# One decay matrix per head: both scan directions summed before the exp, and added before the product

## The chip, the core and the metric

The kernel runs on one core of one Trainium2 chip. The metric is the device time of one execution in microseconds (us). Three runs of the kernel before took 1930.81, 1932.88 and 1936.28 us, with a median of 1932.88 us.

## The reference, cut to what matters

The program has two blocks. The first is a bidirectional state-space (SSD) mixer with a Fourier mixer beside it; the second holds two layers of attention, each followed by an expert-choice feed-forward. The change lies in the SSD scan of the first block. 24 heads in four groups of six scan 256 tokens in two chunks of 128, forward and backward:

```
a_cum = jnp.cumsum(a, axis=-1)          # a = dt * A, per head and direction
lmat = jnp.exp(segsum(a))               # 128 x 128 decays of a chunk, lower triangle, else 0
cb = jnp.einsum('bclgn,bcsgn->bgcls', cc, bc)
y_diag = jnp.einsum('bgcls,bgrcls,bcsgrp->bclgrp', cb, lmat, xc)   # xc = x * dt
...
y_f, h_f = ssd_chunked(xs, dt_f, A[0], bm, cm, h0_f)
y_b, h_b = ssd_chunked(flip(xs), flip(dt_b), A[1], flip(bm), flip(cm), h0_b)
y = y_f + flip(y_b) + d_skip.astype(f32).reshape(g, r)[:, :, None] * xs
```

In unflipped order the forward decays fill one triangle of a head's 128 x 128 matrix and the backward decays the other. The two meet on the diagonal, where both are 1.

## The kernel before, in words

Tokens are on partitions for the scan: a tile [128, ...] holds the 128 positions s of a chunk. `tri` holds four 0/1 triangles. `a` holds dt * A by chunk, direction and head. `cb` holds C B^T of a chunk, masked by each direction's triangle. `mt` holds the decays, and after the masking the matrices that multiply x.

`decay_group` (L746 to L761) builds the decays of a group, per chunk c and direction d:

- L752 multiplies the triangle by `a`, giving six 128 x 128 blocks in a tile `w3` (768 columns), on POOL for forward and on DVE for backward.
- L754 calls `split` (L197): ACT copies the tile into float32r (L203), and the rest is a subtraction (L205) that goes to DVE twice and to POOL once in every three calls. Both parts land in a tile of `hring`, which has four buffers. Every projection of the kernel splits its weights through the same four buffers and the same turn of engines.
- L757 and L758 sum by a product with the triangle `trr`, in two halves of 384 columns and with two parts each, and ACT takes the exp into `mt` (L759).

`ssd_group` (L763) then uses them. `mask` (L785) multiplies `mt` by `cb` on DVE, one instruction of 768 columns per chunk and direction. L799 and L810 make x * dt for both directions on POOL (`weighted`, L768, 768 columns). L825 multiplies per chunk, head and direction, 24 products a group that accumulate two by two in `py`. The compiler turns each of these float32 products into two matmul instructions.

Python generators set the order: `weave` (L851) emits the projections of the next group (`dense_group`) with 1.3 or 1.7 steps of the chain "scan of this group, output part of the group before, decays of the next group" after each of its steps. A scheduler then moves instructions by a simulated timeline, so the final order on each engine is not the written one. The last group is woven with the projections of layer 0's context (`even_dense`), whose input tiles E are written at L450 and L451. Each engine takes its queue in order.

Of the kernel before, what the change touches and what calls it, by code (L numbers as in the profile page):

```python
# [24 lines left out]
F32 = mybir.dt.float32  # L25
# [11 lines left out]
def _constants():  # L37
# [11 lines left out]
    # Fourier: 64-point over the channels of a group, 256-point over the sequence, ortho norm  # L49
# [50 lines left out]
    ex = np.zeros((128, 2, 2, 2), f)   # [kind: query decay, ctx weight][tile][direction]  # L100
# [13 lines left out]
def kernel(ctx, tc, A, out, dbg=None):  # L114
# [14 lines left out]
    def banks(**n):  # L129
        """Split the banks of PSUM anew: tiles of a tag go around its n[tag] banks."""  # L130
# [9 lines left out]
    def psa():  # L140
        return ps_("a")
# [39 lines left out]
    def load_w(src, parts, k0=0, k=8):  # L181
        """A ring tile [128, k, n]: rows (k0..k0+k, p) of src, and its column ranges (c0, n) side by side."""
# [14 lines left out]
    def split(wv):  # L197
        """A part of a ring tile as the sum of two float32r parts."""
# [9 lines left out]
    def mm3(o, l, r, start, stop):  # L208
        """A product of operands in two float32r parts each."""
        mm(o, l[0], r[0], start, False)  # L210
        mm(o, l[0], r[1], False, False)
        mm(o, l[1], r[0], False, stop)
# [6 lines left out]
    def products(wv, outs, first=True, last=True):  # L219
        """Products over the rows of a ring tile; outs: (psum, f), f(k, weights of chunk k) = (stationary, moving)."""  # L220
# [15 lines left out]
    def as_rows(yT, c0, n, k0=0):  # L236
        """f of products: weights' columns c0..c0+127 stationary, the first n tokens of yT moving."""
        return lambda k, w: (cut(w, ALL, slice(c0, c0 + 128)), cut(yT, ALL, k0 + k, n if isinstance(n, slice) else slice(0, n)))

    def as_cols(yT, t, k0=0, c=ALL):  # L240
        """f of products: token tile t of yT stationary, the weights' columns c moving."""
        return lambda k, w: (cut(yT, ALL, k0 + k, slice(128 * t, 128 * t + 128)), cut(w, ALL, c))

# [14 lines left out]
    def tr_at(o, i):  # L258
        """Transpose to other partitions than 0: a product with the identity."""
# [30 lines left out]
    def conditions(i, names, engs):  # L290
        """silu of the two streams' conditions of a pair, as columns."""
# [57 lines left out]
    def ada_early(l, s, slots):  # L349
        """Load the weights of a later modulation step into given slots."""  # L350
# [8 lines left out]
    def ada(src, s, pair, cols, bias, between=None, bank=None, ws=None):  # L359
        """Columns s*512.. of silu(c) @ w + b for both streams of a pair, in chunks of 128: into cols."""  # L360
# [30 lines left out]
    def diag(col, h):  # L391
        """The identity's columns by half h of a gate's columns col [128, 8]: [128, (4, 128)]."""
# [5 lines left out]
    def gate_bcast(o, col, h):  # L398
        """o [128, 512] = half h of a gate on all partitions."""
# [5 lines left out]
    powed = [None]  # L405

    def rstd(ss, n, width, q=None):
        """(ss / width + EPS) ** -0.5"""
# [1411 lines left out]
```

## Time and profile before

| what | value |
|---|---|
| median of three runs | 1932.88 us |
| profiled execution: span from first to last instruction | 1930.3 us |
| PE busy | 1669.9 us (87%) |
| DVE busy | 803.8 us (42%) |
| ACT busy | 520.6 us (27%) |
| POOL busy | 350.4 us (18%) |
| loads from HBM | 554.16 MB, 288 GB/s over the span |

The page gives no time of the profiled execution apart from its span; the three runs lie 0.5 to 6.0 us above that span. The span falls into stages: the first block to about 475 us, layer 0's attention to about 770 us, its experts to 1160 us, layer 1's attention to about 1410 us and its experts to the end. The shares in the table are means over stages that are limited by different things, so the stage that holds the change has to be read by itself.

### The profile page before, as it was taken

To read this page: it belongs to the slowest core of one execution; us is meant where nothing else is said; L and a number is where in the kernel's file an instruction comes from. 1 tells how busy PE (TensorE), PEld (TensorE's weight loads), DVE (VectorE), ACT (ScalarE), POOL (GpSimd) and SP (SyncE) were. 2 spreads that over 40 slices of the span, in tenths; PEclk is the share of its full clock that TensorE was granted. 3 is DMA by queue.
4 is the path that set the end of the run, shared out by engine and by line. 5 is a ranking of instruction groups with operands and counts; after the bars stand their busy time and mean duration, and the time that the engine had idled before them with its cause. 6 is when DMAs were issued, how large, how long until landed. Compare 5 with 4: busy or idle time off the path is not lost.

```text
span 1930.3 us, 29195 instructions
## 1 busy us (share of the span) xinstructions
PE 1669.9 (87%) x12132; PEld 1041.4 (54%) x12132; DVE 803.8 (42%) x1523; ACT 520.6 (27%) x1024; POOL 350.4 (18%) x294
## 2 busy tenths in 40 slices
PE   5999999899999999899989998779998966666665
PEld 4787787799888678433333322268785522222221
DVE  4537788857645664332232121165654300000002
ACT  4334545535443443211210000062532200000001
POOL 3114545553422411000000000032310000000001
PEclk8999999999999999899999999999997976766767
DMA  9566443546566628999989999952287999999996
GB/s 340 194 225 217 159 131 126 184 144 214 190 204 186 210 106 320 355 346 409 409 339 409 410 409 409 407 183 72 90 332 278 408 409 409 409 409 408 409 408 269
DMA packets 223016, 557.11 MB, mean 289 GB/s; under 512 B 23531, under 2 KB 80199, under 8 KB 222884
## 3 DMA queue, kind: packets, MB, share of 16 engines
q1 hardware_dynamic: 216608, 547.92, 75.9%
q10 hardware_dynamic: 5732, 6.26, 1.0%
q8 instruction: 95, 1.56, 0.3%
q0 software_dynamic: 544, 1.06, 0.1%
q14 instruction: 37, 0.30, 0.0%
HBM read 554.16 MB, written 1.05 MB: 288 GB/s over the span
## 4 chain that ended last, share of the span: by engine, by line
PE 59%; DMA 26%; DVE 8%; ACT 3%; issue 2%; POOL 1%; SPq 0%; POOLq 0%; DVEq 0%; ACTq 0%
PE ps_a L149 47%; DMA wm<-in_moe_w_dram 23%; PE ps_b L149 7%; PE ps_b L256 3%; DVE wh L205 2%; DMA w<-in_w_in_dram 1%; PE ps_g L149 1%; DMA w<-in_w_ada_dram 1%; ACT wh L203 1%; DVE pr L1392 1%; DVE ye L1311 1%; DVE hid L1293 0%; DMA w<-in_w_out_dram 0%; DMA w<-in_even_w_in_dram 0%; DVE acc L611 0%
## 5 line engine op out<-in xcount | busy, mean ns | idle before, releaser
L149 PE MATMUL ps_a<-wm,xf 128*32 128x256 f32 (+1 forms) x1792 | 286.4, 575 | 74.6 <-DMA wm<-in_moe_w_dram 72.9
L149 PE MATMUL ps_a<-wm,hidT 128*32 128x256 f32 (+1 forms) x1536 | 204.6, 507 | 45.5 <-DMA wm<-in_moe_w_dram 29.3
L149 PEld LDWEIGHTS ps_a<-wm,xf 128*32 128x32 f32 (+1 forms) x1792 | 91.3, 141 | 259.7 <-issue 131.2
L203 ACT ACTIVATE wh<-w 128x1024 fp32r<-128x1024 f32 (+3 forms) x168 | 165.1, 993 | 177.6 <-PE ps_a L149 104.9
L205 POOL TENSOR_TENSOR wh<-w,wh 128x1024 fp32r<-128x1024 f32 (+3 forms) x56 | 132.3, 2362 | 336.9 <-ACT wh L203 298.3
L205 DVE TENSOR_TENSOR wh<-w,wh 128x1024 fp32r<-128x1024 f32 (+3 forms) x112 | 156.8, 1402 | 73.3 <-ACT wh L203 73.0
L1293 DVE TENSOR_TENSOR hid<-hid,ps_a 128x512 f32<-128x512 f32 (+1 forms) x32 | 17.7, 554 | 382.6 <-PE ps_a L149 382.6
L149 PEld LDWEIGHTS ps_a<-wm,hidT 128*32 128x32 f32 (+1 forms) x1536 | 68.8, 129 | 153.7 <-issue 72.0
L1311 DVE TENSOR_TENSOR ye<-ps_a,SC 32x512 f32<-32x512 f32 (+1 forms) x128 | 70.8, 553 | 184.0 <-PE ps_a L149 182.4
L1210 POOL TENSOR_TENSOR Pg<-Pg,CV 128x128 f32<-128x128 f32 x24 | 9.5, 422 | 750.2 <-DVE Pg L1208 750.2
L1291 ACT ACTIVATE hid<-ps_a 128x512 f32<-128x512 f32 (+1 forms) x32 | 15.7, 489 | 478.7 <-PE ps_a L149 456.6
L149 PE MATMUL ps_a<-hT,wh 128*128 128x512 f32 (+1 forms) x672 | 136.6, 360 | 5.2 <-ACT hT L496 5.1
L149 PEld LDWEIGHTS ps_a<-hT,wh 128*128 128x128 f32 x672 | 111.2, 197 | 24.6 <-ACT hT L496 5.5
L149 PE MATMUL ps_a<-E,wh 128*128 128x256 f32 x768 | 101.3, 286 | 6.5 <-DVE E L451 5.3
L149 PE MATMUL ps_a<-wm,xe 128*32 128x256 f32 (+1 forms) x768 | 104.2, 482 | 0.7 <-ACT hid L1291 0.5
L149 PE MATMUL ps_a<-wh,E 128*128 128x256 f32 (+1 forms) x576 | 99.4, 324 | 2.6 <-DVE wh L205 1.4
L149 PEld LDWEIGHTS ps_a<-E,wh 128*128 128x128 f32 x768 | 94.3, 191 | 12.0 <-DVE E L451 5.9
L149 PEld LDWEIGHTS ps_a<-wh,E 128*128 128x128 f32 x576 | 80.9, 188 | 15.4 <-issue 4.7
L149 PE MATMUL ps_a<-wm,ye 128*32 128x256 f32 x512 | 49.7, 526 | 26.3 <-DMA wm<-in_moe_w_dram 26.3
L611 DVE SCALAR_TENSOR_TENSOR acc<-ps_a,CV,acc 128x189 f32<-128x189 f32 (+2 forms) x160 | 65.8, 426 | 15.6 <-ACT acc L600 13.3
L1011 ACT ACTIVATE pr<-ps_a,nb 128x512 f32<-128x512 f32 (+1 forms) x80 | 47.8, 600 | 79.9 <-DVE nb L1008 71.4
L149 PE MATMUL ps_a<-w,SC 128*32 128x128 f32 x1728 | 65.3, 287 | 3.2 <-DMA w<-in_w_ada_dram 2.1
(522 smaller groups left out, 2430.6 us busy)
## 6 DMA issues: line engine op xcount, KB each, us to landing
wm<-in_moe_w_dram SPq DMA_DIRECT2D x382, 1024.0 KB, 18.3
w<-in_ada_w_dram SPq DMA_DIRECT2D x46, 1024.0 KB, 6.1
w<-in_even_w_in_dram SPq DMA_DIRECT2D x24, 1024.0 KB, 6.9
w<-in_w_ada_dram SPq DMA_DIRECT2D x12, 1024.0 KB, 9.0
w<-in_w_in_dram SPq DMA_DIRECT2D x8, 1024.0 KB, 7.8
w<-in_even_w_out_dram SPq DMA_DIRECT2D x8, 1024.0 KB, 6.4
w<-in_w_in_dram SPq DMA_DIRECT2D x12, 512.0 KB, 7.2
w<-in_w_in_dram SPq DMA_DIRECT2D x8, 768.0 KB, 4.4
```

The costliest lines, as they stand in the source:

```text
L149: PE.matmul(o, l, r, start=start, stop=stop, **kw)
L203: S.activation(hv, wv, AF.Copy)
L205: (G if flip_lo[0] == 0 else V).tensor_tensor(lo, wv, hv, op=OP.subtract)
L256: PE.transpose(o, i, ident[:n, :n])
L611: V.scalar_tensor_tensor(o, xi[:, r0 + dr:r1 + dr, c0 + dc:c1 + dc], tap(i, j), o, op0=OP.mult, op1=OP.add)
L1011: S.activation(pr[:, :n], ps[:, :n], AF.Exp, bias=nb, scale=scale, accum_out=su)
L1210: G.tensor_tensor(g_, g_, bcast(AFF[s][:, t, e4, None], [128, 4, 32]), op=OP.mult)
L1291: S.activation(hid, p1[:, :N], AF.Silu)
L1293: V.tensor_tensor(hid, hid, p3[:, :N], op=OP.mult)
L1311: V.tensor_tensor(ye[o:o + 32, s, N * j:N * j + N], py[i:i + 32, :N], G2[i:i + 32, :], op=OP.mult)
L1392: V.scalar_tensor_tensor(pr[0][0][:, :n], pr[1][0][:, :n], rc, pr[0][0][:, :n], op0=OP.mult, op1=OP.add)
```

## The change

The sums of `a` are split into two float32r parts once, in `ah`, for all groups, instead of splitting each product of `a` with a triangle. POOL multiplies the triangle by the high part, DVE by the low part, straight into an `hring` tile. The sums of both directions accumulate in the same PSUM columns, four products per half, and one exp serves both: one triangle holds the forward decays and the other the backward ones, so `mt` has six blocks per chunk instead of twelve. In `mask`, ACT scales the forward `cb` by dt per head and DVE adds the backward `cb` times its dt, into a tile `w3` of six blocks; one instruction of 768 columns multiplies `mt` by it. The product then takes one matrix per head and x itself; the tiles x * dt and `weighted` on them are gone.

```diff
+    ah = [sp.tile([128, 2, 48], F32R, name=f"ah{i}") for i in range(2)]
...
+        V.tensor_copy(ah[0], a[:, 0:2])
+        V.tensor_tensor(ah[1], a[:, 0:2], ah[0], op=OP.subtract)
...
     def decay_group(g):
         for c in range(2):
+            parts = []
             for d in range(2):
-                w3 = wk.tile([128, 2, 384], F32, name="w3")
-                w = w3.rearrange("p a (r l) -> p (a r) l", l=128)
+                hi_tags.append(hi_tags.pop(0))
+                t = hring.tile([128, 2, 1024], F32R, name="wh", tag=hi_tags[0])
                 h = 24 * d + 6 * g
-                (V if d else G).tensor_tensor(w, bcast(tri[:, d, None, :], [128, 6, 128]),
-                                              bcast(a[:, c, h:h + 6, None], [128, 6, 128]), op=OP.mult)
-                hi, lo = split(w3)
                 for i in range(2):
-                    ps = psa()
-                    mm(ps[:, 0:384], trr[:, d], hi[:, i], start=True, stop=False)
-                    mm(ps[:, 0:384], trr[:, d], lo[:, i], start=False, stop=True)
-                    S.activation(GA["mt"][:, c, 6 * d + 3 * i:6 * d + 3 * i + 3],
-                                 ps[:, 0:384].rearrange("p (a b) -> p a b", a=3), AF.Exp)
-                yield
+                    (V if i else G).tensor_tensor(t[:, i, 0:768].rearrange("p (r l) -> p r l", l=128),
+                                                  bcast(tri[:, d, None, :], [128, 6, 128]),
+                                                  bcast(ah[i][:, c, h:h + 6, None], [128, 6, 128]), op=OP.mult)
+                parts.append(t)
+                if d == 0:
+                    yield
+            for i in range(2):
+                ps = psa()[:, 0:384]
+                n = 0
+                for d in range(2):
+                    for j in range(2):
+                        mm(ps, trr[:, d], parts[d][:, j, 384 * i:384 * i + 384], start=n == 0, stop=n == 3)
+                        n += 1
+                S.activation(GA["mt"][:, c, 3 * i:3 * i + 3], ps.rearrange("p (a b) -> p a b", a=3), AF.Exp)
+            yield
...
         def mask(c):
-            m = GA["mt"][:, c].rearrange("p (d r) l -> p d r l", d=2)
-            for d in range(2):
-                V.tensor_tensor(m[:, d], m[:, d], bcast(cb[:, c, d, None, :], [128, 6, 128]), op=OP.mult)
+            w = wk.tile([128, 2, 384], F32, name="w3").rearrange("p a (r l) -> p (a r) l", l=128)
+            for r in range(6):
+                h = 6 * g + r
+                S.activation(w[:, r], cb[:, c, 0], AF.Copy, scale=dt[:, c, h:h + 1])
+                V.scalar_tensor_tensor(w[:, r], cb[:, c, 1], dt[:, c, 24 + h:25 + h], w[:, r], op0=OP.mult, op1=OP.add)
+            V.tensor_tensor(GA["mt"][:, c], GA["mt"][:, c], w, op=OP.mult)
...
-        xd = {0: weighted(bcast(hd(xs[:, 0])[:, None], [128, 2, 6, 64]), heads(dt[:, 0], g))}
...
-                xd[1] = weighted(bcast(hd(xs[:, 1])[:, None], [128, 2, 6, 64]), heads(dt[:, 1], g))
...
             for r in range(6):
-                for d in range(2):
-                    mm(py[:, 64 * r:64 * r + 64], GA["mt"][:, c, 6 * d + r], xd[c][:, d, 64 * r:64 * r + 64],
-                       start=d == 0, stop=d == 1)
+                mm(py[:, 64 * r:64 * r + 64], GA["mt"][:, c, r], xs[:, c, 64 * r:64 * r + 64])
```

The order of the DMA issues on SP's queue is the same in both kernels. On the other engines the scheduler's order differs in many places from the first group on. Two of them matter below.

The first is DVE's queue at the start of the last group, beside the first tiles E of layer 0's context. Before, E is the float32r remainder that PE's projections wait for (L451), `cb` and `mt` are the masks (L779, L785), and `wh` are the remainders of split weights (L205):

```order
L205 TENSOR_TENSOR wh<-w,wh 128x1024
L448 TENSOR_SCALAR r<-ps_b,MS,M_0_82 128x256
L779 TENSOR_TENSOR cb<-ps_b,kb 128x256 x2
L785 TENSOR_TENSOR mt<-mt,cb 128x768 x3
L205 TENSOR_TENSOR wh<-w,wh 128x1024
L785 TENSOR_TENSOR mt<-mt,cb 128x768
L451 TENSOR_TENSOR E_3446<-r,E_3445 128x512
L804 TENSOR_TENSOR hs<-hs,ps_b 128x384 x2
L817 TENSOR_TENSOR y<-ps_b,ea 128x384
L451 TENSOR_TENSOR E_3446<-r,E_3445 128x512
```

In the changed kernel, L791 is the former L779, L800 the new scaled sum of the two halves of `cb`, and L801 its product with `mt`:

```order
L448 TENSOR_SCALAR r<-ps_b,MS,M_0_82 128x256
L791 TENSOR_TENSOR cb<-ps_b,kb 128x256 x2
L205 TENSOR_TENSOR wh<-w,wh 128x1024 x2
L451 TENSOR_TENSOR E_3410<-r,E_3409 128x512 x2
L800 SCALAR_TENSOR_TENSOR w_3468<-cb,dt,w_3468 128x128 x6
L801 TENSOR_TENSOR mt<-mt,w_3468 128x768
L1353 TENSOR_TENSOR lp<-lp 128x2x64
L800 SCALAR_TENSOR_TENSOR w_3673<-cb,dt,w_3673 128x128
L831 TENSOR_TENSOR y<-ps_b,ea 128x384
L800 SCALAR_TENSOR_TENSOR w_3673<-cb,dt,w_3673 128x128 x5
L205 TENSOR_TENSOR wh<-w,wh 128x1024
L801 TENSOR_TENSOR mt<-mt,w_3673 128x768
```

The four masks that stood ahead of E are gone from there; both halves of E now stand ahead of the new mask of either chunk.

The second is POOL's queue in the first group. Before, `w<-kb,a` is the triangle times `a` (L752), `w<-xs,ws` and `w<-xs,dt` are `weighted` (L768), and `wh<-w` are remainders of splits:

```order
L205 TENSOR_TENSOR wh<-w,wh 128x1024 x2
L205 TENSOR_TENSOR wh<-w,wh 128x768 x2
L752 TENSOR_TENSOR w_1552<-kb,a 128x768
L205 TENSOR_TENSOR wh<-w_1552,wh 128x768
L768 TENSOR_TENSOR w_1620<-xs,ws 128x768
L768 TENSOR_TENSOR w_1622<-xs,ws 128x768
L768 TENSOR_TENSOR w_1701<-xs,ws 128x768
L205 TENSOR_TENSOR wh<-w,wh 128x1024
L768 TENSOR_TENSOR w_1704<-xs,dt 128x768
L798 TENSOR_TENSOR hs<-h_1619,ea 128x768
```

In the changed kernel L759 is the triangle times the high part, and L780 is `weighted`:

```order
L205 TENSOR_TENSOR wh<-w,wh 128x1024 x2
L205 TENSOR_TENSOR wh<-w,wh 128x768
L780 TENSOR_TENSOR w_1608<-xs,ws 128x768
L780 TENSOR_TENSOR w_1610<-xs,ws 128x768
L205 TENSOR_TENSOR wh<-w,wh 128x768
L759 TENSOR_TENSOR wh<-kb,ah_473 128x768 x4
L780 TENSOR_TENSOR w_1701<-xs,ws 128x768
L814 TENSOR_TENSOR hs<-h_1607,ea 128x768
```

The four products of the first group stand in one block behind two `weighted` and a remainder, and one `weighted` is gone.

## Rows read from the trace of the kernel before

**Rows 1.** Stretches: busy us (and instructions) per engine, clock, DMA share, GB/s
```profile
150.00:475.00 325.00, 307.77 (x2133) 262.99 (x2133) 248.62 (x363) 164.60 (x265) 161.20 (x99) 0.97 0.52 165
460.00:770.00 310.00, 301.38 (x2490) 244.02 (x2488) 182.93 (x385) 134.06 (x306) 95.88 (x85) 0.99 0.61 202
770.00:1160.00 390.00, 362.45 (x1635) 137.32 (x1636) 112.57 (x242) 52.62 (x127) 9.06 (x16) 0.98 0.98 386
```

**Rows 2.** The page's chain that ended last, by engine
```profile
PE 59%; DMA 26%; DVE 8%; ACT 3%; issue 2%; POOL 1%; SPq 0%; POOLq 0%; DVEq 0%; ACTq 0%
```

**Rows 3.** PE's waits from 150 to 475 us: total us, times, longest
```profile
PE ps_a L149 <- DVE E L451: 4.9, 1, 4.9
PE ps_b L256 <- DVE gy L833: 3.9, 4, 1.6
PE ps_a L149 <- ACT mt L759: 3.5, 2, 3.3
```

**Rows 4.** PE in order of time: start us, us, instructions
```profile
203.08 2.79 PE L149 MATMUL ps_b<-w,mt 128*128 128x64 f32 x24
```

**Rows 5.** Line L752 of the kernel: ns min/median/max, first and last start
```profile
L752 POOL TENSOR_TENSOR w<-kb,a x8: 1467/1472/1472, 83.9 to 356.5; 128x768 f32<-128x768 f32 x8
L752 DVE TENSOR_TENSOR w<-kb,a x8: 942/1104/2554, 84.3 to 366.4; 128x768 f32<-128x768 f32 x8
```

**Rows 6.** Groups by form, 150 to 475 us, DVE and POOL
```profile
L611 DVE SCALAR_TENSOR_TENSOR acc<-ps_a,CV,acc 128x189 f32<-128x189 f32 x64 | 25.7, 408 | 13.4 <-ACT acc L600 12.8
...
L785 DVE TENSOR_TENSOR mt<-mt,cb 128x768 f32<-128x768 f32 x16 | 25.4, 1615 | 1.1 <-ACT mt L759 1.0
L205 DVE TENSOR_TENSOR wh<-w,wh 128x768 fp32r<-128x768 f32 x22 | 25.1, 1142 | 8.8 <-ACT wh L203 8.8
...
L205 POOL TENSOR_TENSOR wh<-w,wh 128x768 fp32r<-128x768 f32 x10 | 19.2, 1924 | 31.1 <-ACT wh L203 31.1
...
L768 POOL TENSOR_TENSOR w<-xs,dt 128x768 f32<-128x768 f32 x8 | 16.1, 2010 | 5.5 <-PE ps_b L256 2.8 <-PE ps_b L149 2.7
...
L374 DVE TENSOR_TENSOR M<-ps_b,BC 128x8 f32<-128x8 f32 x8 | 1.3, 163 | 6.9 <-PE ps_b L256 6.9
```

**Rows 7.** Groups by form, 150 to 475 us, ACT
```profile
L203 ACT ACTIVATE wh<-w 128x768 fp32r<-128x768 f32 x32 | 26.7, 844 | 22.5 <-PE ps_a L149 10.7 <-DMA w<-in_w_in_dram 6.9 <-POOL w L752 3.6
...
L759 ACT ACTIVATE mt<-ps_a 128x384 f32<-128x384 f32 x32 | 14.9, 499 | 1.8 <-PE ps_a L149 1.5
...
L759 ACT ACT_TABLE_LOAD x5 | 6.4, 1283 | 0.1
...
L841 ACT ACTIVATE xg<-ps_b,VC 128x256 fp32r<-128x256 f32 x12 | 4.9, 477 | 1.2 <-PE ps_b L256 0.7 <-PE ps_a L149 0.5
...
L156 ACT ACTIVATE ra<-ps_a 128x128 f32<-128x128 f32 x4 | 1.1, 267 | 2.1 <-PE ps_a L149 2.1
```

**Rows 8.** DVE in order of time, 369 to 390 us
```profile
374.89 4.71 DVE L785 TENSOR_TENSOR mt<-mt,cb 128x768 f32<-128x768 f32 x3
...
381.94 2.23 DVE L785 TENSOR_TENSOR mt<-mt,cb 128x768 f32<-128x768 f32 x1
384.09 2.82 DVE L451 TENSOR_TENSOR E<-r,E 128x512 fp32r<-128x512 f32 x1
```

**Rows 9.** PE in order of time, where the second group's projections begin
```profile
174.10 6.88 PE L149 MATMUL ps_a<-hT,wh 128*128 128x512 f32 x28
```

**Rows 10.** POOL in order of time, first group
```profile
158.01 1.85 POOL L205 TENSOR_TENSOR wh<-w,wh 128x768 fp32r<-128x768 f32 x1 [5.83 <-ACT wh L203]
...
163.19 1.84 POOL L205 TENSOR_TENSOR wh<-w,wh 128x768 fp32r<-128x768 f32 x1 [0.96 <-ACT wh L203]
```

**Rows 11.** SP's queue: first loads of the experts' weights
```profile
726.97 4.68 SPq L1241 DMA_DIRECT2D wm<-in_moe_w_dram  x6
```

**Rows 12.** What SP's queue waited for, 470 to 800 us
```profile
SPq L1241 <- PE ps_a L149: 41.1, 11, 13.7
```

**Rows 13.** DVE in order of time, first group
```profile
163.30 2.55 DVE L752 TENSOR_TENSOR w<-kb,a 128x768 f32<-128x768 f32 x1
```

More of the change, by code (lines that the diff above doesn't have):

```diff
@@ L873, in open_wm @@
         GA["wm"] = enter(b1, name="b1m", bufs=1, reuse_waits="tile")
-        GA["mt"] = GA["wm"].tile([128, 2, 12, 128], F32, name="mt")
+        GA["mt"] = GA["wm"].tile([128, 2, 6, 128], F32, name="mt")
         yield
```

## The prediction

> **What bounds the kernel now.** I first read the busy time by stretches, to see which engine fills the stage that holds the change. From 150 to 475 us, where all four groups are scanned, PE is busy 307.77 of 325 us, at a granted clock of 0.97 and a DMA share of 0.52; DVE is busy 248.62 us, ACT 164.60 and POOL 161.20 [rows 1]. So the stage is PE's, DVE comes second, and DMA has room. The chain that ended last says the same of the whole program: PE holds 59% of it, DMA 26%, DVE 8% [rows 2]. PE's waits in this stage come next, since idle PE is the only other thing that can be won here. All its idle time is 325 - 307.77 = 17.2 us. The largest single wait is 4.9 us for E, DVE's remainder of layer 0's context; four waits for the normalized output gy make 3.9 us, and two for the exps 3.5 us, of which one is 3.3 us [rows 3].
>
> **PE's work.** Before, a group has 24 products of `mt` with x * dt, and each is two instructions; 24 instructions, that is one chunk, took 2.79 us [rows 4]. The change halves them: 12 instructions fewer in each of 4 x 2 chunks, 96 in all. At 2.79 / 24 = 0.116 us each they are 11.2 us. PE's sums with `trr` stay 64 instructions in number; only their grouping in PSUM differs. As PE is full around these products, I count the 11.2 us in whole. If PE had to wait there for something else, they would be worth nothing: 0 to -11.2.
>
> **DVE, POOL and ACT.** DVE loses 16 masks of 1.615 us (25.8), 8 triangle products (median 1.104 us, 8.8), and of the subtractions of 768 columns 13 of 22 by the order (13 x 1.142 = 14.8) [rows 5, 6]: 49.4 us. It gains 16 triangle products (17.7), 8 full masks (8 x 1.615 = 12.9), 48 small sums of 128 columns, and three subtractions of 1024 columns, because the turn of `split` shifts; I price these at no less than the 768 columns' 1.142 (3.4). The trace has no such small sum. The nearest rows are 408 ns for 189 columns of the same operation and 163 ns for 8 columns of an addition [rows 6], so 7.8 to 19.6 us for all; by columns between them, 0.326 us and 15.6 us. DVE gains 49.6 us: even, with ends of -8 and +4.
>
> POOL loses 8 triangle products (1.472), 8 `weighted` on dt (2.010) and 3 remainders of 768 columns (1.924), 33.6 us, and gains 16 products, 23.6 us: 10 us less [rows 5, 6]. ACT loses 16 copies of 768 columns (0.844) and 16 exps (0.499), 21.5 us, and gains 48 scaled copies of 128 columns. The nearest are 267 ns for a plain copy of 128 and 477 ns for 256 with a scale per partition [rows 7]; I take 0.36, 17.3 us, with ends of 12.8 and 22.9. None of this sets the end by itself. It matters only where PE waits, and I go through those places.
>
> **The wait for E goes.** Ahead of E, DVE does three masks in 4.71 us, a remainder, and the fourth mask in 2.23, and only then E, at 384.09 [rows 8]. In the changed order both halves of E stand ahead of either mask. E is ready 4.71 + 2.23 = 6.9 us sooner on DVE, and PE's wait of 4.9 [rows 3] is shorter than that, so I count -4.9. What is late next is POOL's and ACT's part of E, on engines that lose work; and if the group's two new products on DVE run long, the wait stays in part: 0 to -4.9. The masks that move behind E are then needed by the scan's products, and PE has projections in between.
>
> **The first group.** Here PE's wait of 3.3 us for an exp [rows 3] falls, and its run of projections of the second group starts at 174.10 [rows 9]. Before, each decay passes four steps (product, copy, remainder, sum); now two. But now all four high parts stand in one block on POOL behind two `weighted` and a remainder. From 158.0, where POOL's remainder starts before [rows 10], this is 2 x 2.010 + 1.924 + 4 x 1.472 = 11.8 us [rows 5, 6], so until 169.8; PE's last sums with `trr` and their exps come about 2 us later. I take a start of 172, -2 us, with ends of 0 (every product slowed to the 2.01 of `weighted`, +2.2) and -4.
>
> **What it adds.** The order has two more loads of ACT's function table, at 1.283 us each [rows 7], both in the second group, ahead of the exps and of gy's part. Fewer copies and exps stand beside them, so I count +1 of 2.6. There the wait for gy is already the second largest [rows 3]. The Trainium skill, "ScalarE: Activation LUTs", section "What ACT_TABLE_LOAD costs", puts a switch at 2.66 us with the drain; by that the two would be up to 5.3 us and the sum 2.7 us later at most, while the row shows the load alone. Further, a tile of `hring` is now held from the forward product to the end of both directions' sums, where projections need the same four buffers: +1, with an end of +9 that stands among the rivals.
>
> **The sum.** -11.2 - 4.9 - 2 + 1 + 1 = -16.1 us. The profiled execution would go from a span of 1930.3 to 1914.2; the median of the runs lies 2.6 us above the span, so I predict 1917 us.
>
> The later stages should pass the gain on. Layer 0's attention is PE's too, 301.38 of 310 us with a DMA share of 0.61, and the experts' loads that fill the next stage (DMA 0.98) [rows 1] are first issued at 726.97 [rows 11], by a line whose longest waits are for PE, 41.1 us [rows 12]; they begin as much sooner as PE gets there.
>
> **Rivals.**
>
> *All of PE's idle time in the stage closes too.* POOL's relief speaks for it, gy's wait against it, since gy hangs on a chain of DVE, ACT and POOL that keeps its length. -11.2 - 17.2 = -28.4: 1904.5 us.
>
> *The held buffers give half of it back.* A projection's split must then wait for a sum of both directions. One late split costs PE a copy and a remainder, 0.844 + 1.924 = 2.8 us by [rows 6, 7], at most; half of that in each of the six woven chunks is +9 over my +1 less: 1917 + 8 = 1925 to 1926. The order, which puts the next projections' copies ahead of exps in places, speaks for it; the four buffers and PE's long runs against it.
>
> *DVE and POOL block each other: slower.* The high and low products of a direction become ready together, and both engines read SBUF for them. Before, one DVE product took 2.55 us [rows 13] while POOL worked on a remainder [rows 10], against 0.942 us at best [rows 5]. If all the new pairs ran like this, the 12 DVE products of the three stretches in which DVE stands before PE (the first group, the third's start, the fourth's start) grow by 12 x (2.55 - 1.10) = 17.4 us. The wait for E then stays, as do 2 us for loads and buffers and 3 us of the small sums' upper end: -11.2 + 17.4 + 2 + 0 to 3 = +8 to +11, 1941 to 1944 us. It decides against any gain from a mean of about 1.9 us per product: 9.2 / 12 above 1.10. POOL's 10 us less and the median of 1.104 beside much POOL work speak against it. The Trainium skill, "SBUF — State Buffer", section "Who interferes with whom", says that a DVE instruction with two SBUF inputs contends with a GpSimd instruction that reads SBUF and that the later one is blocked entirely; the row of 2.55 us agrees, and the rule speaks for this rival.
>
> *It doesn't reach the end.* The experts' loads could hang on something that doesn't move with PE, and the stage full of DMA would then start as before: 1932 us. SP's waits for PE [rows 12] speak against it.
>
> **How the numbers follow.** A measurement of this kernel can tell about 0.3%, 5.8 us, from no change: faster is below 1927.1, slower above 1938.7. The forecast (1911 to 1923) gets 0.55, all idle closed 0.10, the held buffers 0.20, of which a third lands within 0.3%, blocking 0.10, and no effect at the end 0.05. Faster: 0.55 + 0.10 + 0.13 = 0.78; same: 0.07 + 0.05 = 0.12; slower 0.10. The range of 1905 to 1931 leaves out the slower rival and little else.
>
> **What would show it.** In the profile after: products of x with `mt`, 12 instructions in about 1.4 us; PE's wait for E gone; the second group's projections at about 172; DVE's products of `ah` at a mean under 1.9 us; the first load of experts' weights near 711. Wrong would be PE idle by much more than 17 us between 150 and 460, with waits for DVE or POOL at the decays, or the first expert load at 727 as before.

## The result, and the profile after

The changed kernel takes 1910.32 us (median of four runs, 1906.99 to 1914.0) where the kernel before, on the same chip, takes 1934.58 us. The ratio is 0.9877, with a 95% interval of 0.9852 to 0.9901. A second measurement of the changed kernel on another chip gave 0.9896 (0.9873 to 0.9919). It is faster by 20 to 24 us; the forecast was 16. The profiled span goes from 1930.3 to 1905.1 us.

The busy time by stretches, as in [rows 1]: the stretch from 150 to 475 us, then layer 0's attention and its experts.

```profile
150.00:475.00 325.00, 307.56 (x2160) 264.75 (x2159) 262.73 (x423) 174.37 (x300) 156.42 (x98) 0.98 0.54 176
460.00:770.00 310.00, 298.34 (x2466) 236.45 (x2465) 176.41 (x407) 125.44 (x297) 86.18 (x80) 0.98 0.63 215
770.00:1160.00 390.00, 364.49 (x1573) 132.08 (x1571) 104.86 (x209) 48.05 (x115) 9.05 (x16) 0.99 0.98 387
```

PE is as full as before. Since the program now is some 18 us ahead there, the first window holds more work of layer 0, so it can't be subtracted from [rows 1]; lengths between the same instructions can, and a table below gives them. DVE has 262.73 us where it had 248.62, but most of that is the later work: up to the scan's end, the first product of `dg` with `ones`, DVE is busy for 282.8 us before (at 428.6 us) and 286.2 after (at 410.4). The chain that ended last is the same in kind as in [rows 2]:

```profile
PE 60%; DMA 26%; DVE 8%; ACT 3%; issue 2%; POOL 1%; SPq 0%; DVEq 0%; POOLq 0%; ACTq 0%
```

PE's waits from 150 to 475 us, as in [rows 3] (total us, times, longest):

```profile
PE ps_a L149 <- DVE wh L205: 6.1, 4, 2.5
PE ps_b L149 <- DVE hs L819: 3.3, 2, 1.7
PE ps_a L149 <- DVE E L451: 1.8, 2, 1.3
PE ps_b L256 <- DVE gy L845: 1.8, 2, 1.5
PE ps_a L149 <- ACT E L450: 1.8, 2, 0.9
PE ps_a L149 <- POOL wh L759: 1.7, 2, 1.3
```

The one wait of 4.9 us for E and the one of 3.3 us for an exp are gone. In their place stand shorter waits for split weights (`wh`), for the states' sums `hs` and for both parts of E. The products of x with one matrix per head, against [rows 4]; the start of the second group's projections, against [rows 9]; and SP's first load of experts' weights, against [rows 11]:

```profile
197.83 1.45 PE L149 MATMUL ps_b<-xs,mt 128*128 128x64 f32 x12
```
```profile
168.53 1.86 PE L149 MATMUL ps_a<-hT,wh 128*128 128x512 f32 x7
```
```profile
706.98 3.12 SPq L1253 DMA_DIRECT2D wm<-in_moe_w_dram  x6
```

Groups by form, 75 to 475 us on DVE and POOL, 150 to 475 us on ACT, against [rows 5 to 7] (count | busy us, mean ns | idle before):

```profile
L800 DVE SCALAR_TENSOR_TENSOR w<-cb,dt,w 128x128 f32<-128x128 f32 x48 | 32.5, 737 | 0.0
L759 DVE TENSOR_TENSOR wh<-kb,ah 128x768 fp32r<-128x768 f32 x16 | 24.3, 1526 | 0.4 <-PE ps_a L149 0.4
L801 DVE TENSOR_TENSOR mt<-mt,w 128x768 f32<-128x768 f32 x8 | 7.6, 955 | 0.2
...
L759 POOL TENSOR_TENSOR wh<-kb,ah 128x768 fp32r<-128x768 f32 x16 | 32.3, 2039 | 6.2 <-PE ps_a L149 6.2
...
L799 ACT ACTIVATE w<-cb,dt 128x128 f32<-128x128 f32 x48 | 14.9, 391 | 3.9 <-DVE mt L801 2.6 <-PE ps_b L149 1.3
L772 ACT ACT_TABLE_LOAD x6 | 7.7, 1283 | 0.1
```

The 48 small sums (L800) take 32.5 us. The means of this view can hold more than an instruction's own work, so the same line by itself, with minimum, median and maximum in ns:

```profile
L800 DVE SCALAR_TENSOR_TENSOR w<-cb,dt,w x48: 337/347/2498, 166.3 to 377.5; 128x128 f32<-128x128 f32 x48
```

Of the 48, 33 take 0.34 to 0.35 us. The other 15 take 0.60 to 2.50, and by the single records each of these 15 ends 0.14 to 0.15 us behind the end of a POOL instruction (in x0 it is 15 of 15 again). The largest case is seen in time. DVE and POOL at the last group's first mask:

```profile
364.85 7.65 DVE L800 SCALAR_TENSOR_TENSOR w<-cb,dt,w 128x128 f32<-128x128 f32 x6
372.54 0.96 DVE L801 TENSOR_TENSOR mt<-mt,w 128x768 f32<-128x768 f32 x1
...
377.80 1.21 DVE L205 TENSOR_TENSOR wh<-w,wh 128x1024 fp32r<-128x1024 f32 x1
...
380.14 1.00 DVE L819 TENSOR_TENSOR hs<-hs,ps_b 128x384 f32<-128x384 f32 x2
```
```profile
364.34 1.50 POOL L394 TENSOR_TENSOR dg<-kb,M 128x512 f32<-128x512 f32 x1
365.80 1.34 POOL L451 TENSOR_TENSOR E<-r,E 128x512 fp32r<-128x512 f32 x1
367.10 1.09 POOL L394 TENSOR_TENSOR dg<-kb,M 128x512 f32<-128x512 f32 x1
368.15 2.46 POOL L205 TENSOR_TENSOR wh<-w,wh 128x1024 fp32r<-128x1024 f32 x1
370.57 1.53 POOL L814 TENSOR_TENSOR hs<-h,ea 128x768 f32<-128x768 f32 x1
```

Six sums of 0.35 us take 7.65, as long as five POOL instructions back to back: the first five end with one POOL instruction each (the fourth runs from 368.26 to 370.76, POOL's remainder beside it from 368.15 to 370.61), and the sixth, with POOL idle, takes 0.34. In the first group six took 7.46 us from 166.27, beside POOL; the next six, with POOL idle, took 1.66:

```profile
176.98 1.66 DVE L800 SCALAR_TENSOR_TENSOR w<-cb,dt,w 128x128 f32<-128x128 f32 x6
```

### The profile page after: what moved, and what is told of

Same layout as the page of the kernel before. It is cut to its first block, busy times and chain, and to the rows that moved or that the text cites. A ratio compares the mean times of both kernels' runs of the same rounds, so it can differ in the third digit from the quotient of the medians.

```text
span 1905.1 us, 29062 instructions
## 1 busy us (share of the span) xinstructions
PE 1652.3 (87%) x12036; PEld 1026.2 (54%) x12036; DVE 794.4 (42%) x1563; ACT 519.3 (27%) x1042; POOL 335.1 (18%) x288
## 4 chain that ended last, share of the span: by engine, by line
PE 60%; DMA 26%; DVE 8%; ACT 3%; issue 2%; POOL 1%; SPq 0%; DVEq 0%; POOLq 0%; ACTq 0%
PE ps_a L149 48%; DMA wm<-in_moe_w_dram 22%; PE ps_b L149 7%; PE ps_b L256 3%; DMA w<-in_w_in_dram 2%; DVE w L800 1%; PE ps_g L149 1%; DMA w<-in_w_ada_dram 1%; DVE wh L205 1%; ACT wh L203 1%; DMA w<-in_w_out_dram 1%; DVE ye L1323 1%; DVE pr L1404 1%; DVE hid L1305 1%; DVE acc L614 1%
## 5 line engine op out<-in xcount | busy, mean ns | idle before, releaser
L149 PE MATMUL ps_a<-wm,xf 128*32 128x256 f32 (+1 forms) x1792 | 280.0, 558 | 73.6 <-DMA wm<-in_moe_w_dram 71.8
L149 PE MATMUL ps_a<-wm,hidT 128*32 128x256 f32 (+1 forms) x1536 | 211.8, 529 | 47.4 <-DMA wm<-in_moe_w_dram 31.7
L203 ACT ACTIVATE wh<-w 128x1024 fp32r<-128x1024 f32 (+3 forms) x152 | 151.7, 1007 | 164.6 <-PE ps_a L149 99.9
L1305 DVE TENSOR_TENSOR hid<-hid,ps_a 128x512 f32<-128x512 f32 (+1 forms) x32 | 17.7, 555 | 375.2 <-PE ps_a L149 375.2
L205 POOL TENSOR_TENSOR wh<-w,wh 128x1024 fp32r<-128x1024 f32 (+3 forms) x50 | 116.0, 2321 | 304.4 <-ACT wh L203 278.5
L205 DVE TENSOR_TENSOR wh<-w,wh 128x1024 fp32r<-128x1024 f32 (+3 forms) x102 | 135.2, 1329 | 71.9 <-ACT wh L203 71.4
```

The costliest lines, as they stand in the source:

```text
L149: PE.matmul(o, l, r, start=start, stop=stop, **kw)
L203: S.activation(hv, wv, AF.Copy)
L205: (G if flip_lo[0] == 0 else V).tensor_tensor(lo, wv, hv, op=OP.subtract)
L1305: V.tensor_tensor(hid, hid, p3[:, :N], op=OP.mult)
```

## The experiments

The x runs were timed in five rounds beside the kernel before. The lengths (us) come from one profile each, as differences between the starts of the same four events: c_n's load on SP, the start of the second group's projections, the first transpose of c_n on PE, and the first product of `dg` with `ones` behind the scan (before: 155.8, 174.1, 369.2, 428.6). The four together are the scan's stage; "first", "middle" and "last" are its parts.

| kernel | ratio to before (95%) | first | middle | last | stage |
|---|---|---|---|---|---|
| before | 1 | 18.3 | 195.1 | 59.4 | 272.8 |
| x5, new turn in before | 0.9974 (0.9956 to 0.9993) | 18.2 | 194.9 | 59.8 | 273.0 |
| after | 0.9877 (0.9852 to 0.9901) | 15.9 | 183.8 | 58.1 | 257.8 |
| x0, after again | 0.9896 (0.9873 to 0.9919) | 16.0 | 183.4 | 58.6 | 257.9 |
| x4, old turn after scan | 0.9897 (0.9879 to 0.9916) | 15.8 | 185.2 | 58.5 | 259.4 |
| x1, products twice | 0.9940 (0.9922 to 0.9958) | 16.0 | 189.2 | 62.8 | 268.0 |
| x2, decays alone | 0.9940 (0.9921 to 0.9959) | 16.0 | 191.0 | 61.7 | 268.8 |
| x3, products alone | 1.0007 (0.9986 to 1.0029) | 18.1 | 191.8 | 60.6 | 270.4 |
| x6, states before mask | 0.9927 (0.9908 to 0.9946) | 16.1 | 186.4 | 57.2 | 259.7 |
| x7, low and high on DVE | 0.9913 (0.9895 to 0.9932) | 14.1 | 190.0 | 57.0 | 261.1 |
| x8, first group on DVE | 0.9911 (0.9890 to 0.9932) | 14.0 | 190.7 | 58.0 | 262.8 |
| x9, own tile | 0.9891 (0.9872 to 0.9911) | 14.6 | 189.6 | 51.3 | 255.5 |
| x10, no small sums | 0.9867 (0.9843 to 0.9891) | 16.1 | 181.7 | 50.1 | 247.9 |
| x12, sum on POOL | 0.9906 (0.9880 to 0.9933) | 15.6 | 183.6 | 53.3 | 252.5 |

The pairs with the same code up to there (before and x5; after, x0 and x4) agree within 0.2 and 1.7 us, so a difference of 2 us or more in the stage is taken as one of the kernel.

**x0, the changed kernel again.** No edit.

> The changed kernel once more, beside the others on one chip, with a second profile. All theories: 1907 to 1914 us. If the 2.9 us by which its profile was ahead before 150 us, where no instruction of the change runs, are the clock's doing and not the change's, this profile has them in part or not at all; if they are the order's, they are there again.

1910.43 us, and the stage's 257.9 us repeats the first profile's 257.8. The lead ahead of the scan is there again too: c_n's load comes at 152.4 us (155.8 before, 152.7 in the first profile). That does not make it the order's, since x5, whose code there is that of before, has it as well (152.8).

**x1, every product twice.**

```diff
+                for _ in range(2):
-                mm(py[:, 64 * r:64 * r + 64], GA["mt"][:, c, r], xs[:, c, 64 * r:64 * r + 64])
+                    mm(py[:, 64 * r:64 * r + 64], GA["mt"][:, c, r], xs[:, c, 64 * r:64 * r + 64])
```

> The changed kernel with each of its 48 products of x with the decay matrix issued twice into the same columns, the second overwriting the first: 96 matmul instructions more, nothing else written differently. Theory A (PE's instructions in this stage count in full): 96 x 0.116 = 11.2 us slower than the changed kernel, 1921 to 1922 us. Rival B (the gain comes from waits around the decays, and PE has slack at the products): 0 to 3 us slower, 1910 to 1913 us. Rival C (the gain comes from the scheduler's other order): the order moves again, so anything between 1905 and 1935, and not the same as A by more than chance.

1919.08 us, 8.7 over the changed kernel; the stage grows by 10.2. PE's busy time in its middle and last part:

```profile
168.50:352.30 183.80, 175.90 (x1260) 144.82 (x1259) 159.50 (x293) 95.81 (x169) 88.06 (x59) 0.99 0.49 156
352.30:410.40 58.10, 52.34 (x349) 47.41 (x348) 40.96 (x52) 30.76 (x55) 32.21 (x21) 0.94 0.54 177
```
```profile
168.50:357.70 189.20, 182.23 (x1330) 151.35 (x1330) 160.86 (x294) 95.68 (x169) 87.50 (x59) 1.00 0.47 151
357.70:420.50 62.80, 57.39 (x374) 52.22 (x373) 38.14 (x50) 30.89 (x55) 32.93 (x21) 0.89 0.49 166
```

The first pair is the changed kernel, the second x1: 70 and 25 instructions more, 6.3 and 5.1 us more of PE; in the last part some of this is the lower clock (0.89 against 0.94). This is theory A, if short of its 11.2: the products reach the end nearly in whole, once everything else is as in the changed kernel.

**x2, the new decays alone.** Masks per direction and x * dt as before, so 24 products a group.

```diff
+            for d in (1, 0):
+                V.tensor_tensor(GA["m2" if d else "mt"][:, c], GA["mt"][:, c], bcast(cb[:, c, d, None, :], [128, 6, 128]), op=OP.mult)
...
+                for d in range(2):
+                    mm(py[:, 64 * r:64 * r + 64], GA["m2" if d else "mt"][:, c, r], xd[c][:, d, 64 * r:64 * r + 64], start=d == 0, stop=d == 1)
```

> The new decay_group alone: parts of a split once, both directions in one sum, one exp per half. The mask multiplies by each direction's masked C B^T as before (two instructions of 768 columns), and the products stay 24 a group on x * dt. A: 8 to 13 us faster than before (what is left of 24 us without PE's 11.2), 1921 to 1927 us. B: nearly all of the gain, 1910 to 1916 us. C: no pattern. Nothing is left out of the computation.

1918.74 us, by the ratio 11.6 us faster than before (7.9 to 15.3), as A has it. But the stage is only 4.0 us shorter; in the profile 6.5 us lie behind it, where x2 has the new turn of `split` too (see x4 and x5). The first part has all of the changed kernel's gain (16.0 us). In the last, PE waits 6.8 us for E in one piece, more than before.

**x3, the products alone.** Decays as before, their two directions multiplied on DVE before the new mask (eight more instructions of 768 columns).

```diff
+            m = GA["mt"][:, c]
+            V.tensor_tensor(m[:, 0:6], m[:, 0:6], m[:, 6:12], op=OP.mult)
+            V.tensor_tensor(m[:, 0:6], m[:, 0:6], w, op=OP.mult)
```

> The old decay_group (two directions, each split and summed and its exp taken by itself), then one matrix per head: DVE multiplies the two directions' decays (8 instructions of 768 columns more than in the changed kernel), and the new mask and the 12 products a group follow. A: 96 matmul instructions fewer than before, 11 us, less up to 4 us where DVE's 8 instructions of about 1 us are waited for: 1920 to 1926 us. B: within 4 us of before, 1930 to 1935 us.

1930.92 us, no change, as B has it; the stage is 2.4 us shorter. (Its profiled execution had a granted clock of 0.82 from 635 to 700 us, where before had 0.99, so nothing is read from it behind the stage.) In the middle part PE has 7.8 us less work than before and the part is 3.3 us shorter: PE now waits, 4.9 us for hs and 4.4 for the exps between 130 and 475 us. x2 and x3 save 4.0 and 2.4 us, both parts together 15.0. So the two parts help each other. Why is not separated: x3 gives DVE 16 instructions a group (twelve sums, two products of the decays, two masks) for four masks, and its DVE is busy for 224.5 us of the stage (211.0 before, 215.7 in the changed kernel), but ACT has 15 us more than before as well.

**x4 and x5, the turn of `split`.** Behind 428 us the changed kernel gained 7.0 us more in its profile (3.9 in x0's). The change takes 16 splits out, so each later remainder falls on the engine that its predecessor's had. x4 sets the changed kernel's turn back to that of before, x5 gives the kernel before the new one.

```diff
     weave(chain(ssd_group(3), out_group(2), out_group(3)), gen_c, 0.8, 0)
+    flip_lo[0] = (flip_lo[0] + 1) % 3    # x4; + 2 in x5
```

> The changed kernel with the turn of `split` set forward by one step once, behind the scan, so that from layer 0 on each remainder goes to the engine that it has in the kernel before; the first block keeps its order. Theory A, the turn: the change takes 16 splits out of the turn, so later remainders change engine, and that gives the 4 to 7 us that the changed kernel gains behind 428 us; then this kernel keeps the 18 us gained by 428 us and loses the 4 to 7: 1914 to 1918 us on a chip where the changed kernel takes 1910. Theory B, the gain behind 428 us is only the first block's gain read against loads that land at other times: within 2 us of the changed kernel.

> The kernel before with the turn of `split` set forward by two steps once, behind the scan (two forward is one back, as the change makes it), and nothing else. Theory A, the turn alone: 4 to 7 us faster than before, about 1925 us, with the same times as before up to 428 us. Theory B, the turn is worth nothing: 1931 us, within 2 us of before. Its first block is that of the kernel before, so its trace up to 428 us also shows how far two profiles of that block differ.

x4 took 1912.59 us, nearest to its theory B; x5 1926.16, by the ratio 5.0 us faster than before (1.4 to 8.5), as its theory A has it, except that its profile is ahead by 3 us at c_n's load already. The place can be shown: layer 1's attention, from PE's first product of the experts' outputs `ye` to its first product of the router (`kb` with `xT`). In order: before, x4 (old turn), x5, after (new turn).

```profile
1258.40:1446.60 188.20, 178.90 (x1112) 143.84 (x1113) 112.35 (x191) 81.00 (x161) 49.49 (x47) 0.98 0.46 164
```
```profile
1240.50:1426.70 186.20, 176.16 (x1114) 141.66 (x1114) 111.98 (x191) 80.77 (x161) 49.36 (x47) 0.99 0.47 166
```
```profile
1254.70:1436.80 182.10, 175.11 (x1114) 140.78 (x1114) 104.11 (x191) 81.17 (x161) 48.84 (x47) 1.00 0.48 170
```
```profile
1238.80:1422.00 183.20, 176.22 (x1114) 141.64 (x1114) 104.19 (x191) 81.10 (x161) 48.72 (x47) 0.99 0.48 169
```

PE has the same work in all four (1112 to 1114 instructions). At the same granted clock of 0.99 and the same busy time of 176.2 us the new turn is 3.0 us shorter (183.2 against 186.2): PE idles 7.0 us instead of 10.0. The rest of the spread goes with the clock. All eleven profiles with the new turn lie between 181.8 and 185.7 us, the three with the old one between 186.2 and 188.6. So about 3 us are the turn's. From the first product of `ye` to the end x4 is 3.5 to 3.8 us longer than x0 and the changed kernel (670.1 against 666.6 and 666.3); between the scan and that product it is 3.4 and 0.6 us shorter (827.8 against 831.2 and 828.4), for which no cause is shown. That x4 lost no time over the whole run is within its interval (-16 to -23 us against before), so more than these 3 us is not settled.

**x6, the states before the mask.** The first `mask(0)` is written behind the sums of `hs`.

> The changed kernel with the first chunk's mask written behind the states' sums (hs) instead of ahead of them. Theory A, DVE's new masks stand ahead of hs and this made the wait that took E's place: PE's waits for hs (3.3 us in two) go, the stretch from 352 to 410 us gets 2 to 4 us shorter, 1906 to 1909 us where the changed kernel takes 1910. Theory B, the waits only move once more, to the mask or gy: within 2 us of the changed kernel, with a wait for mt or gy of about 3 us.

1918.05 us, by the ratios 6 to 10 slower than the changed kernel. The last part is 1 us shorter (57.2), but the middle is 2.6 us longer and new waits of 3.5 us for `acc` appear. In the last part the waits are still there: 2.4 us for `wh` and 1.5 for hs, where the changed kernel has 2.5 and 1.7. The edit changed the written order, but on DVE's queue the small sums of both chunks still stand ahead of hs:

```profile
368.66 7.13 DVE L800 SCALAR_TENSOR_TENSOR w<-cb,dt,w 128x128 f32<-128x128 f32 x7 [0.76 <-ACT w L799]
...
377.78 2.95 DVE L800 SCALAR_TENSOR_TENSOR w<-cb,dt,w 128x128 f32<-128x128 f32 x3
...
382.66 1.01 DVE L817 TENSOR_TENSOR hs<-hs,ps_b 128x384 f32<-128x384 f32 x2
```

So x6 does not test theory A.

**x7 and x8, the triangle products on DVE alone**, in all groups (x7) or the first (x8):

```diff
-                    (V if i else G).tensor_tensor(t[:, i, 0:768].rearrange("p (r l) -> p r l", l=128),
+                    (V if i or g == 0 else G).tensor_tensor(t[:, i, 0:768].rearrange("p (r l) -> p r l", l=128),
```

> The changed kernel with both products of the triangle with `ah` on DVE, none on POOL, so that the two engines no longer work on the same decays at once. Theory A, PE is full and the pairs are hidden: DVE has 16 x 0.94 = 15 us more of work, POOL 16 x 2.18 = 35 us less, and the time stays within 3 us of the changed kernel. Theory B, the pairs that slow each other (1.56 us on DVE and 2.18 on POOL where the shortest are 0.94 and 1.47) cost PE time: 3 to 6 us faster, above all in the first group, whose projections of the second start 1 to 2 us sooner. Theory C, DVE's queue is what PE waits for: 3 to 8 us slower, with more waits for DVE's wh and hs.

> The changed kernel with the first group's triangle products all on DVE (x7's edit for this group alone); the other three groups keep POOL for the high parts. Theory A, in the first group PE waits for the pair of engines, and later DVE has no room: the first group's part of x7's result stays (there the second group's projections started 1.8 us sooner against the load of c_n) and its loss behind that goes, so 1 to 2 us faster than the changed kernel, 1909 to 1911 us where before takes 1932. Theory B, the loss of x7 is the first group's: 3 to 4 us slower, 1915 us.

x7 1915.87, x8 1915.28 us. In x7 DVE's products fall to a median of 948 ns (from 1564): the pairs do slow each other, DVE's product by two thirds. In both runs the first part is 1.8 to 1.9 us shorter, as theory B of x7 says, but this is not a gain. The first part of the changed kernel, then of x7:

```profile
152.70:168.50 15.80, 14.19 (x73) 12.04 (x71) 15.23 (x19) 8.52 (x19) 15.11 (x8) 1.00 0.84 289
```
```profile
154.00:168.10 14.10, 11.87 (x61) 10.15 (x59) 13.64 (x18) 7.15 (x12) 5.42 (x3) 0.99 0.92 321
```

PE does 12 instructions and 2.3 us of work less in x7's (x8's has 62 instructions); they now stand behind the second group's first projection, where its middle and last part have 7 and 5 instructions more. Over the whole stage x7 is 3.3 us longer and x8 5.0. So taking POOL out of the pairs gains nothing here. A loss at the end is likely but not shown: the intervals overlap with x0's, and both profiles are of the slowest of six executions. x8's theory A is not borne out; its time is that of theory B.

**x9, the forward parts in a tile of their own.**

```diff
-                t = hring.tile([128, 2, 1024], F32R, name="wh", tag=hi_tags[0])
+                t = GA["wm"].tile([128, 2, 768], F32R, name="dp")     # for d = 0
```

> The changed kernel with the forward decays' two parts in a tile of their own instead of one of hring's four buffers, so that the tile that is held longest no longer keeps a buffer from the projections. Theory A, the held buffer costs the +1 us of the forecast or less: within 1.5 us of the changed kernel. Theory B, PE's waits for wh (6.1 us in four, where before had 4.4 in two) come from that buffer: 2 to 5 us faster, with these waits under 3 us.

1912.27 us, the same. PE's waits for `wh` fall from 6.1 to 1.2 us (before had 1.4 in one between 150 and 475 us, not the 4.4 of the expectation), and others come up (gy 3.5, hs 2.5, acc 2.4). The stage is 2.3 us shorter (its middle and last part can't be read apart from each other, since the transposes of c_n moved back in PE's order). So theory B's waits are right and its gain is not: the held buffer makes waits, but costs no time that shows at the end.

**x10, without the small sums.**

```diff
-            for r in range(6):
-                ...
-            V.tensor_tensor(GA["mt"][:, c], GA["mt"][:, c], w, op=OP.mult)
+            V.tensor_tensor(GA["mt"][:, c], GA["mt"][:, c], bcast(cb[:, c, 0, None, :], [128, 6, 128]), op=OP.mult)
```

> The changed kernel without the 48 scaled copies on ACT and the 48 small sums on DVE: `mt` is multiplied by the forward `cb` alone, in one instruction per chunk (the backward direction and dt are left out of the product). DVE loses 48 x 0.337 = 16 us, ACT 48 x 0.389 = 19 us, PE nothing. Theory A, this work lies beside PE's, as the forecast had it: within 2 us of the changed kernel. Theory B, the last group's waits for hs, wh and E (5.7 us between 352 and 410 us), which took the place of the wait for E, are DVE's small sums: 3 to 5 us faster, in that stretch.

1907.12 us, and the stage is 9.9 us shorter, 8.0 of it in the last part, where theory B looked, and twice as much as it said. (The profile is of the fastest of its four executions.) By the ratios 2 to 6 us of it are left at the end, but its interval overlaps with those of x0 and the changed kernel. The kernel leaves out ACT's 48 scaled copies together with the sums, so by itself it does not tell the two apart; x12 does. The last part of x10:

```profile
352.10:402.20 50.10, 47.97 (x350) 43.75 (x349) 33.56 (x40) 27.15 (x43) 31.69 (x20) 1.00 0.58 193
```

PE does 350 instructions there, the changed kernel 349. Idle goes from 58.10 - 52.34 = 5.8 to 2.1 us, and the same work takes 4.4 us less, at a granted clock of 1.00 instead of 0.94. Where the clock fell in the changed kernel (375 to 390 us in steps of 5), and x10 there:

```profile
375.00:380.00 5.00, 2.05 (x16) 1.64 (x14) 5.00 (x6) 1.38 (x2) 2.21 (x1) 1.00 0.00 0
380.00:385.00 5.00, 3.71 (x16) 3.31 (x17) 4.21 (x7) 0.00 (x0) 1.84 (x1) 0.68 0.33 87
385.00:390.00 5.00, 5.00 (x30) 5.00 (x30) 1.11 (x2) 0.95 (x1) 1.89 (x3) 0.63 0.79 283
```
```profile
375.00:380.00 5.00, 5.00 (x42) 4.74 (x42) 4.93 (x4) 1.13 (x2) 3.04 (x2) 1.00 0.20 54
380.00:385.00 5.00, 5.00 (x38) 4.47 (x37) 2.13 (x3) 1.99 (x5) 2.65 (x3) 1.00 0.93 331
385.00:390.00 5.00, 5.00 (x45) 5.00 (x44) 2.09 (x4) 2.24 (x3) 3.66 (x3) 1.00 0.00 0
```

DVE is busy all through 375 to 380 us while PE stands for 3 of 5 us, waiting for `wh` (2.5 us) and then `hs` (1.7), both queued on DVE behind the sums. From 380 to 390 us PE then has 0.68 and 0.63 of its clock, that is 1.2 GHz for most of the ten microseconds. So these waits are paid about twice. It is not a rule for every wait: in x9 PE waits 2.5 us for hs in the last part, at a granted clock of 1.00.

**x12, the last group's sums on ACT and POOL.** ACT scales the backward `cb` too, into a second tile u, for the last group.

```diff
+                    S.activation(u[:, r], cb[:, c, 1], AF.Copy, scale=dt[:, c, 24 + h:25 + h])
+                G.tensor_tensor(w, w, u, op=OP.add)
```

> The changed kernel, complete in what it computes, but in the last group the six small sums per chunk go from DVE to ACT and POOL: ACT scales the backward `cb` too (six more copies of 128 columns at 0.389 us per chunk), and POOL adds the two tiles in one instruction of 768 columns (about 2 us); DVE only multiplies. The first three groups keep their order. Theory A, in the last group DVE's small sums stand ahead of hs and wh, which PE waits for: DVE loses 12 x 0.337 = 4 us there, the waits of 2.5 and 1.7 us go and with them the drop of the granted clock to 0.65 behind them; the stretch of 58 us goes to 50 to 54 us, as without the sums (50.1 us), and the time to 4 to 6 us under the changed kernel, 1905 to 1908 us where before takes 1932. Theory B, ACT's and POOL's longer chain to the mask only moves the wait to mt, and the stretch stays at 57 to 59 us: within 2 us of the changed kernel.

The stretch goes as theory A has it: 53.3 us, with waits of 1.0 us at most and a granted clock of 1.00. ACT has twelve copies more here than in the changed kernel, so it is DVE's sums, not ACT's copies, that made the waits.

```profile
352.90:406.20 53.30, 50.39 (x359) 45.47 (x358) 35.99 (x39) 34.01 (x68) 36.58 (x24) 1.00 0.54 176
```

The time does not follow: 1912.77 us, from 1905.11 to 1923.16 over six runs. Its profiled execution is the fastest of the six (span 1903.2). No version is shown to beat the changed kernel; where the 5 us go in the other executions is open.

## Why the prediction was right, and where not

The forecast was 1917 us and the measured time is 1910.32. It lies inside the range of 1905 to 1931, but 0.7 us below the band of 1911 to 1923 that got a chance of 0.55.

**PE's work** (-11.2 us): right. Doubling the products costs 10.2 us in the stage and 11.4 us of PE's busy time. But this gain hangs on the rest of the change: with the old decays and the new mask (x3) the stage is 2.4 us shorter, not 11.

**The wait for E** (-4.9 us): the step that failed. The wait went as the order said, E was ready early, yet the last part is only 1.3 us shorter (0.8 in x0), with a quarter of the products' gain in it as well. The sentence that the masks behind E "are then needed by the scan's products, and PE has projections in between" left out what else stands behind them on DVE: hs and the next remainders. And the prices were off. The small sums were put at 15.6 us with an upper end of 19.6; they take 32.5, the triangle products 24.3 instead of 17.7 for 16, the masks less than forecast (7.6 instead of 12.9). DVE's total still comes near the forecast's even, 3.4 us more up to the end of the scan, so it is not the amount of DVE's work that failed but where it stands: 11.5 us of sums (from 364.85 to 377.9 us) in one queue ahead of `wh` and hs. x10 and x12 show the cost where it lands: without the sums on DVE this part is 8.0 and 4.8 us shorter. At the end of the run neither gain is clear of the noise.

**The rival on DVE and POOL** was placed on the wrong line. Its bound was a mean of 1.9 us per triangle product; that mean is 1.53, and the rival did not come true. The same mechanism struck at the small sums, which the forecast priced by columns alone. From 364.85 us six of them last as long as POOL's five instructions beside them. By the Trainium skill, "SBUF — State Buffer", section "Who interferes with whom", a DVE instruction with two SBUF inputs contends with a GpSimd instruction that reads SBUF, over a shared pair of ports that is an exclusive lock. The trace agrees, with 2.5 us for a sum of 0.35 behind a POOL instruction of 2.46, and with all 15 long sums ending where a POOL instruction ends.

**The first group** (-2 us): right, -2.4, the size in part by luck. POOL's block takes 14.3 us (153.39 to 167.67) where 11.8 were forecast, its four products 2.2 us each, which the forecast had as the end worth 0:

```profile
153.39 2.92 POOL L780 TENSOR_TENSOR w<-xs,ws 128x768 f32<-128x768 f32 x2 [4.05 <-ACT xs L734]
156.27 2.56 POOL L205 TENSOR_TENSOR wh<-w,wh 128x768 fp32r<-128x768 f32 x1
158.78 8.89 POOL L759 TENSOR_TENSOR wh<-kb,ah 128x768 fp32r<-128x768 f32 x4
```

But the block begins sooner (0.7 us behind c_n's load, where the forecast had 2.2), and PE starts 0.9 us behind it instead of 2. PE's granted clock in this part is also 1.00 where before and x5 have 0.91. The start at 168.53 is 3.5 us earlier than the 172 forecast, but 3.2 of it lie ahead of the decays, and x5, whose code there is that of before, has 3.1 of them.

**Loads and buffers** (+2 us): too high, as far as is seen. The two table loads are there (13 instead of 11 at all lines from 150 to 475 us). x9 finds no cost of the held buffers in the time. The middle part is 11.3 us shorter, where three quarters of the products and these two terms make 8.4 - 2 = 6.4. The 5 us more come with the new decays: x2, without the halved products, is 4.1 us shorter in the middle, and the sum had counted no gain there. How they come is open. Against before the gain is all in PE's busy time (188.11 to 175.90 us; idle 7.0 and 7.9), some of it the clock's (0.97 and 0.99). Against x5, at the same clock of 0.99 as x2, it is in part idle time: 9.8 us in x5, 7.9 in the changed kernel, 6.3 in x2.

**The sum**: -16.1 forecast, -15.0 in the stage, with errors of +6.4 in the last part (-1.3 for -4.9 - 2.8) and -4.9 in the middle that nearly cancel, which is luck. What makes 20 to 24 of it lies outside the stage: 3 us of the turn of `split` in layer 1, which the forecast saw in the counts of subtractions and did not follow further; and 2 to 6 us that these runs don't settle. In the profiles the changed kernel gains nothing clear between the scan and layer 1's attention (829.8 us before; 828.4 and, in x0, 831.2), and 5.6 and 5.3 us from the first product of `ye` to the end (671.9 us before).

**The other rivals.** Not all idle closed: in the middle and last part PE idled 12.5 us before and 13.7 after. The gain did reach the end: the first expert load is at 706.98, where 711 was forecast.

## What to carry to other kernels

Price a new instruction on DVE not by its columns alone but by what POOL runs beside it: many short instructions with two SBUF inputs are the worst case, since each may wait for a whole POOL instruction. When a wait is about to go, read the queue of the engine that ended it down to the next things that PE needs, and look at the granted clock behind the wait, since it can cost as much again. Taking calls out of a round-robin (here 16 from a turn of three) moves the later calls to other engines, and that is part of the change. When the start of a later piece of work moves, count the instructions ahead of it before calling it a gain.

## What the runs showed of the hardware that was not expected

Six sums of 128 columns took 1.66 us with POOL idle and 7.65 beside it. POOL is held up as well: its triangle products take 1469 ns at best, 2181 in the median.

PE at a faster clock does not always make a stretch shorter: before and x5 run the same code in the middle part, with PE busy for 188.11 and 185.07 us, at 0.97 and 0.99, in 195.1 and 194.9 us. And the same code can have another clock in another execution: from 60 to 75 us before was granted 0.89 and x5 1.00, and x5 arrived 3 us sooner at c_n's load.

```profile
60.00:75.00 15.00, 15.00 (x119) 10.41 (x118) 3.91 (x7) 1.43 (x4) 0.08 (x1) 0.89 0.43 148
```
```profile
60.00:75.00 15.00, 15.00 (x135) 11.02 (x135) 5.13 (x12) 2.81 (x5) 0.00 (x0) 1.00 0.63 209
```
